# Full-row second matmul for the neighbourhood scores, and modulation sums on the vector engine

## The chip, the cores and the metric

The kernel runs on one core of a Trainium2 chip. The metric is device time in microseconds (us) of one execution, median of several runs. The core's engines work side by side, each through a queue of its own in order: PE (TensorE, matmuls; "PEld" is its weight load), DVE (VectorE), ACT (ScalarE), POOL (GpSimd) and SP (which here only issues transfers). They wait for each other by semaphores.

## The reference

One layer of a diffusion backbone over 512 latent tokens and 256 context tokens of 1024 channels. Cut to what the change touches:

```python
sh1, sc1, g1, sh2, sc2, g2 = adaln(c, w_mod, b_mod)      # split of silu(c) @ w_mod + b_mod, w_mod 1024 x 6144
hx = modulate(rmsnorm(x, norm_attn_g), sh1, sc1)         # the first 2048 columns: shift and scale
...
# neighbourhood attention, 8 heads of 64: window of 8 x 16 tokens with a learned bias, and all context keys
s = einsum('bqhd,bjkhd->bhqjk', qr, kr) * scale + bias   # masked outside the window
s_ctx = einsum('bqhd,bchd->bhqc', qr, k_ctx) * scale
p = softmax(concatenate([s, s_ctx]))
...
x = x + g1 * mixed                                       # columns past 2048: g1, sh2, sc2, g2
hx2 = modulate(rmsnorm(x, norm_ffn_g), sh2, sc2)
x = x + g2 * hierarchical_moe(hx2, ...)
```

## The kernel before

The program runs in stages: norms and projections of the tokens (to about 113 us), neighbourhood attention in four pairs of heads (p = 0 to 3, to about 268 us), latent attention, output projection with router, then 16 experts whose weights stream in, and the last norm. Up to the experts a scheduler sets the order of the instructions on each engine from the order of the code and its own estimates; the experts' order is written by hand.

**Neighbourhood scores.** A pair has 2 heads (u) and 4 blocks of 128 queries (i), 32 blocks in all. Matmuls in full precision are made of high and low parts: `qh` holds the high part of a head's queries twice (rows 0 to 63 and 64 to 127), `kk` the keys' high part (rows 0 to 63) and low part (rows 64 to 127). So the first matmul of `na_scores` (L599) gives high x high + high x low over 128 rows, and the second (L600) adds low queries x high keys over 64 rows, `ql[0:64]` and `kk[0:64]`. A block's 512 columns come in one to three pieces. DVE then adds the mask (L605) and takes the row maximum (L469), ACT takes the exponent (L612), PE transposes the weights (L621), DVE or ACT copies them (L81, L83). Scores have two banks in turn. Between these steps PE works off the projections of the next pair (`pull`: L56 to L58, three matmuls for each product), in pair 3 the latent heads' values.

**Modulation sums.** `mod_rest(n)` runs after every second block, 16 times: it loads two tiles `raw` of `w_mod_b` (128x1024 each, a ring of three buffers that the weights `w_qk`, `w_ukv` and `w_uq` share, all issued on SP) and lets PE add the product of 128 rows of silu(c) (`sstat`, 32 columns of which one counts) with 4 x 512 columns to a bank, in four groups of 32 columns of the array (L520). After 8 calls a row of 2048 columns is complete; DVE adds the bias (L524), SP stores it to `mod_d`. The latent attention's stage reads the gate g1 from there first.

Of the kernel before, what the change touches and what calls it, by code (L numbers as in the profile page):

```python
# [13 lines left out]
OP = mybir.AluOpType  # L14
# [16 lines left out]
# columns of the constant pack  # L31
# [6 lines left out]
def hybrid_kernel(tc, nc, x_k, x_q, ctx, cvec, w_mod_a, w_mod_b, b_mod_c, b_mod_r, g_ffn_row,  # L38
# [25 lines left out]
    # low parts that wait for their turn on the vector engine  # L64
# [22 lines left out]
    def rstd_steps(out, ss, n, n_cols, wk, first=None):  # L87
        """1 / sqrt(ss / n + eps): the root of the scalar engine, and one Newton step on its inverse.
        Of a sum in two parts the first one comes earlier."""
# [25 lines left out]
    # ------------------------------------------------------------ constants and small parameters  # L115
# [31 lines left out]
    # ------------------------------------------------------------ pools of the first phases  # L147
# [4 lines left out]
    # the tokens come in the places of the attentions' results  # L152
# [12 lines left out]
    # the root's table, ahead of its use  # L165
# [35 lines left out]
    def bank(*nums):  # L201
        """A bank of the sums' memory, of those named in turn."""
        n = taken[nums] = taken.get(nums, -1) + 1
        return psA.tile([P, 512], F32, name="ps", tag=f"b{nums[n % len(nums)]}", bufs=1)
# [8 lines left out]
    # ------------------------------------------------------------ modulated norm of the tokens, channel-major  # L213
# [24 lines left out]
    def mod_sums(q):  # L238
        """Shift and scale of two channel tiles, for latent and context tokens."""
# [14 lines left out]
    def mod_first(c):  # L254
        """The same of one of the first two channel tiles."""
# [90 lines left out]
    # ------------------------------------------------------------ latents of keys and values, of queries  # L346
# [30 lines left out]
    # what leaves for the memory lies apart from what follows  # L377
# [49 lines left out]
    # ------------------------------------------------------------ ring of the experts' weights  # L427
# [17 lines left out]
    def load_experts(n, behind=None):  # L445
        """Starts the loads of the next n chunks of experts' weights, in the order of their use."""
        for i in range(len(loads), min(len(loads) + n, len(order))):
# [6 lines left out]
            # few in flight, so that the small transfers between them don't queue for long  # L454
# [7 lines left out]
    # ------------------------------------------------------------ neighbourhood attention  # L462
# [3 lines left out]
    def row_max(s):  # L466
        """A block's row maximum, negated."""
        nm = cst.tile([P, 1], F32, name="nm", tag="nm", bufs=8)
        ve.tensor_reduce(out=nm, in_=s, axis=AX.X, op=OP.max, negate=True)  # L469
        return nm  # L470

    def softmax_block(s, pr, ssum):
        """exp of a block of scores less their row maximum, and the row sums."""
        ac.activation(pr, s, AF.Exp, bias=row_max(s), accum_out=ssum)

    def normalise_steps(ssum, wk, hi, lo):
        """Divides a pair of heads' sums by their rows' sums, which are turned into rows on the way."""
# [21 lines left out]
    # the sums of the experts' rows, by tokens  # L499
# [4 lines left out]
    # the other modulations, as rows  # L504
    mod_d = tc.dram_tile([2, 4, 512], F32, name="mod_d")
    modf = mod_d.rearrange("r a b -> r (a b)")
    mod_ps = []

    def mod_rest(n):
        r, k = divmod(n, KT)  # L510
        if k == 0:
            br = nw.tile([P, 512], F32, name="br", tag="br", bufs=1)
# [3 lines left out]
            mod_ps[:] = bank(7), br, rows  # L516
        ps, br, rows = mod_ps
        ws = [load(w_mod_b[r, k, :, q * 1024:(q + 1) * 1024]) for q in range(2)]
        for g in range(4):
            pe.matmul(ps[g * 32:(g + 1) * 32, :], sstat[:, k, :],  # L520
                      ws[g // 2][:, g % 2 * 512:g % 2 * 512 + 512], start=(k == 0), stop=(k == KT - 1),
                      tile_position=(0, g * 32))
        if k == KT - 1:
            ve.tensor_tensor(br, br, ps, op=OP.add)  # L524
            sy.dma_start(mod_d[r], rows)

    na_heads, na_w, na_ps = {}, {}, {}

    def na_open(p):
        heads = na_heads[p] = []  # L530
        for u in range(2):
            qh = nw.tile([P, T], F32R, name="qh", tag="qh", bufs=4)
            ql = nw.tile([P, T], F32R, name="ql", tag="ql", bufs=4)
# [9 lines left out]
    def na_bias(p, u):  # L543
        """The bias of a head, with the window's mask."""
# [4 lines left out]
    def na_weights(p, j, i):  # L549
        """The high part (i = 0) and the low one (1) of the weights of queries (j = 0) or keys (1)."""  # L550
# [8 lines left out]
    def na_project(p, j):  # L559
        """Queries (j = 0), latent keys (1) or context's keys (2) of a pair of heads. Yields between the steps."""  # L560
# [9 lines left out]
    def na_part(p, j, u, i):  # L570
        """Their high part (i = 0) and low one (1), of a head."""
# [16 lines left out]
    def na_scores(p, u, i):  # L588
# [9 lines left out]
        for o, n, c in pieces:  # L598
            pe.matmul(s[:, o:o + n], qh[:, qs], kk[:, c:c + n], start=True, stop=False)  # L599
            pe.matmul(s[:, o:o + n], ql[0:64, qs], kk[0:64, c:c + n], start=False, stop=True)  # L600
# [13 lines left out]
    def na_turn(p, u, i):  # L614
        """A block's weights by keys."""
# [32 lines left out]
    # ------------------------------------------------------------ latent attention  # L648
# [9 lines left out]
    def mla_values(t):  # L658
        """Values of the latent heads, and the queries' weights and latents in two parts. Yields between the steps."""
# [29 lines left out]
    for j in range(3):  # L689
        for n, _ in enumerate(na_project(0, j)):  # L690
# [4 lines left out]
            if n == 4 and j == 1:  # L695
                na_weights(1, 0, 0)
                na_weights(1, 0, 1)
                # the table of exp, ahead of its use
# [102 lines left out]
    def halves(n):  # L801
        """Two banks for sums of 1024 columns, by halves."""
# [11 lines left out]
    def k_rope(b):  # L814
        """The part of the keys that the heads share."""
        split_later(khs[b][64:96, :], kls[b][64:96, :], krt[64:96, :])

    def queries(a, ts=range(4)):
        """Queries of four heads."""
# [18 lines left out]
    def k_prep(p, hf):  # L838
        """Keys of a pair of heads, of the latent tokens (hf = 0) or the context's (1)."""
# [1058 lines left out]
```

## Time and profile before

| | |
|---|---|
| median of 3 runs | 760.02 us (759.91 to 760.87) |
| span of the profiled execution | 759.4 us |
| PE busy | 721.5 us (95%) |
| DVE busy | 546.4 us (72%) |
| ACT busy | 446.0 us (59%) |
| POOL busy | 77.8 us (10%) |

The span runs from the first to the last instruction of one profiled execution; the median of the runs without a profile is 0.6 us above it. Busy shares are over the whole span; they differ by stage, which the rows further down show. A record's length holds an engine's latency too, so instructions of one engine that follow each other closely overlap in the rows: what an instruction costs is the distance from its start to the next one's start. Rows of windows give the engines in the order PE, PEld, DVE, ACT, POOL.

### The profile page before, as it was taken

How to read it: one execution, taken by the hardware profiler on the slowest of the kernel's cores; microseconds unless marked ns; L12 is line 12 of the kernel's file. 1: busy time of each engine (PE TensorE's matmuls, PEld its weight loads, DVE VectorE, ACT ScalarE, POOL GpSimd, SP SyncE). 2: the span in 40 equal slices, each digit the busy share in tenths (PEclk: the TensorE clock that was granted, in tenths of full speed). 3: DMA queues.
4: the chain of work that ended last, by engine and by line, in shares of the span. 5: the costliest groups of instructions: out<-in, count | busy, mean ns of one | idle time of the engine just before them, and what ended most of it. 6: DMA issues, size and time to landing. Idle time of an engine off the chain costs nothing. (4 is left out here: it accounts for less than half of the span.)

```text
span 759.4 us, 10561 instructions
## 1 busy us (share of the span) xinstructions
PE 721.5 (95%) x3982; PEld 527.0 (69%) x3983; DVE 546.4 (72%) x744; ACT 446.0 (59%) x697; POOL 77.8 (10%) x46
## 2 busy tenths in 40 slices
PE   4999999999999999999999929999999999999995
PEld 4679987666665588776666826777777777777773
DVE  5572465646565589474564758999999999999996
ACT  6452364444434466464583428777777777777773
POOL 1000000000000000000000001033222322221220
PEclk9999999999999999999999958999999999999998
DMA  8931237544446662031139968999999999999872
GB/s 324 406 99 49 83 131 244 187 146 146 140 140 220 182 227 85 28 112 42 43 144 345 339 231 309 351 377 371 356 361 367 368 354 359 364 355 384 309 131 110
DMA packets 39621, 176.94 MB, mean 233 GB/s; under 512 B 5288, under 2 KB 6768, under 8 KB 27280
## 3 DMA queue, kind: packets, MB, share of 16 engines
q1 hardware_dynamic: 35168, 164.24, 58.6%
q0 software_dynamic: 4112, 11.92, 7.4%
q8 instruction: 32, 0.52, 0.3%
q14 instruction: 21, 0.17, 0.1%
q10 hardware_dynamic: 288, 0.08, 0.0%
HBM read 163.00 MB, written 15.32 MB: 235 GB/s over the span
## 5 line engine op out<-in xcount | busy, mean ns | idle before, releaser
L1356 DVE TENSOR_TENSOR el<-ew,eh 128x2048 fp32r<-128x2048 f32 (+1 forms) x106 | 220.5, 2087 | 20.7 <-ACT eh L1353 13.4
L1353 ACT CAST eh<-ew 128x1024 fp32r<-128x1024 f32 x190 | 189.7, 1048 | 43.2 <-PE s L58 28.6
L56 PE MATMUL s<-eh,xh 128*96 128x512 f32 x260 | 104.4, 401 | 0.9 <-ACT xh L61 0.9
L58 PE MATMUL s<-eh,xl 128*96 128x512 f32 x260 | 102.8, 396 | 0.0
L57 PE MATMUL s<-el,xh 128*96 128x512 f32 x260 | 102.4, 394 | 0.0
L1567 POOL DMA_INDIRECT ya_d<-yo,idx x14 | 45.5, 3253 | 140.4 <-DVE yo L1571 140.4
L58 PEld LDWEIGHTS s<-eh,xl 128*96 128x96 f32 x260 | 42.2, 162 | 19.1 <-DVE xl L62 0.6
L56 PEld LDWEIGHTS s<-eh,xh 128*96 128x96 f32 x260 | 42.2, 162 | 17.9 <-ACT xh L61 1.2
L57 PEld LDWEIGHTS s<-el,xh 128*96 128x96 f32 x260 | 42.3, 163 | 17.3 <-DVE el L1356 0.2
L56 PE MATMUL y<-eh,ghh 128*96 128x512 f32 x120 | 48.2, 401 | 0.0
L58 PE MATMUL y<-eh,ghl 128*96 128x512 f32 x120 | 47.3, 394 | 0.0
L57 PE MATMUL y<-el,ghh 128*96 128x512 f32 x120 | 47.2, 393 | 0.0
L56 PE MATMUL ps<-wh,hh 128*128 128x512 f32 (+2 forms) x128 | 43.8, 345 | 0.4 <-ACT hh L274 0.3
L469 DVE TENSOR_REDUCE nm<-s 128x1 f32<-128x768 f32 x32 | 30.5, 954 | 19.0 <-PE s L58 18.7
L58 PE MATMUL ps<-wh,hl 128*128 128x512 f32 (+2 forms) x128 | 43.5, 345 | 0.3 <-DVE hl L276 0.3
L57 PE MATMUL ps<-wl,hh 128*128 128x512 f32 (+2 forms) x128 | 43.3, 341 | 0.0
L1284 POOL MEMSET xg<- 128x1024 f32 x2 | 1.8, 950 | 388.0 <-DMA g<-mod_d 388.0
L605 DVE TENSOR_TENSOR ps<-ps,bb 128x256 f32<-128x256 f32 x32 | 13.8, 432 | 35.1 <-PE ps L600 35.0
L56 PE MATMUL ps<-hh,wh 128*128 128x512 f32 (+1 forms) x96 | 38.7, 403 | 0.0
L1242 POOL DMA_INDIRECT xg<-hx_d,idx x16 | 23.6, 1475 | 118.9 <-DVE va L1165 50.5
L933 ACT ACTIVATE pr<-s,nm 128x768 f32<-128x768 f32 x32 | 29.0, 908 | 9.6 <-DVE nm L469 9.3
L58 PE MATMUL ps<-hh,wl 128*128 128x512 f32 (+1 forms) x96 | 34.5, 359 | 0.0
(357 smaller groups left out, 1501.4 us busy)
## 6 DMA issues: line engine op xcount, KB each, us to landing
ew<-w_gate SPq DMA_DIRECT2D x32, 1024.0 KB, 9.3
ew<-w_up SPq DMA_DIRECT2D x32, 1024.0 KB, 9.2
ew<-w_down SPq DMA_DIRECT2D x32, 1024.0 KB, 9.3
raw<-w_mod_b SPq DMA_DIRECT2D x32, 512.0 KB, 3.8
wm<-w_mod_a SPq DMA_DIRECT2D x16, 512.0 KB, 9.2
raw<-w_qk SPq DMA_DIRECT2D x8, 512.0 KB
ya_d<-zero SPq DMA_DIRECT2D x10, 256.0 KB, 7.5
raw<-w_v SPq DMA_DIRECT2D x4, 512.0 KB
```

The source lines that it names most:

```text
L56: pe.matmul(ps, lh, rh, start=start, stop=False)
L57: pe.matmul(ps, lh, rl, start=False, stop=False)
L58: pe.matmul(ps, ll, rh, start=False, stop=stop)
L469: ve.tensor_reduce(out=nm, in_=s, axis=AX.X, op=OP.max, negate=True)
L605: ve.tensor_tensor(s[:, 0:256], s[:, 0:256], bb[:, 1 if i == 3 else 0, :], op=OP.add)
L933: ac.activation(pr, s, AF.Exp, bias=nm, accum_out=mla_ssum[h // 2][:, t, h % 2:h % 2 + 1])
L1242: ins = gp.indirect_dma_start(out=xg[e % NX][slice(0, CAP), :], out_offset=None, in_=hx_d, in_offset=bass.IndirectOffsetOnAxis(ap=idx[slic ...
L1284: gp.memset(x_, 0.0)
L1353: ac.copy(wh[:, cs], r[:, cs])
L1356: ve.tensor_tensor(wl[:, cs], r[:, cs], f(wh[:, cs]), op=OP.subtract)
L1567: gp.indirect_dma_start(out=ya_d, out_offset=bass.IndirectOffsetOnAxis(ap=idx[rows, 1, e:e + 1], axis=0), in_=yo[rows, :], in_offset=None, ...
```

## The change

Two edits. First, the low parts of the queries get four buffers of their own, `qls`, whose rows 64 to 127 POOL sets to zero once, and the second matmul of the scores runs over all 128 rows of `ql` and `kk` (L617 in the new numbering; the zeros cancel the keys' low part). Second, the columns of `w_mod` past 2048 are laid out in eight groups of 512. For each group DVE multiplies the 8 row tiles with their value of silu(c) by row and adds them up in `macc` (L529, L531), two half groups to the 16 calls; then four small matmuls with a matrix of ones (L535) sum over the rows, DVE adds the bias (L537) and SP stores 512 columns. `br` is 128 columns wide in place of 512, and `mod_d` is written eight times in place of two. The comments of the file went, too.

```diff
-    mod_d = tc.dram_tile([2, 4, 512], F32, name="mod_d")
-    modf = mod_d.rearrange("r a b -> r (a b)")
+    mod_d = tc.dram_tile([8, 4, P], F32, name="mod_d")
+    modf = mod_d.rearrange("(h r) a b -> h (r a b)", h=2)
     mod_ps = []
+    macc = nw.tile([P, 512], F32, name="macc")
+    ones = nw.tile([P, 32], F32, name="ones")
+    ve.memset(ones, 1.0)
 
     def mod_rest(n):
-        r, k = divmod(n, KT)
-        if k == 0:
-            br = nw.tile([P, 512], F32, name="br", tag="br", bufs=1)
+        r, h = divmod(n, 2)
+        if h == 0:
+            br = nw.tile([P, P], F32, name="br", tag="br", bufs=1)
             ve.memset(br, 0.0)
             rows = br.rearrange("(a b) n -> a b n", b=32)[:, 0, :]
             sy.dma_start(rows, b_mod_r[r])
-            mod_ps[:] = bank(7), br, rows
-        ps, br, rows = mod_ps
-        ws = [load(w_mod_b[r, k, :, q * 1024:(q + 1) * 1024]) for q in range(2)]
-        for g in range(4):
-            pe.matmul(ps[g * 32:(g + 1) * 32, :], sstat[:, k, :],
-                      ws[g // 2][:, g % 2 * 512:g % 2 * 512 + 512], start=(k == 0), stop=(k == KT - 1),
-                      tile_position=(0, g * 32))
-        if k == KT - 1:
-            ve.tensor_tensor(br, br, ps, op=OP.add)
+            mod_ps[:] = br, rows
+        br, rows = mod_ps
+        for k2 in (2 * h, 2 * h + 1):
+            w = load(w_mod_b[r, k2])
+            for i in range(2):
+                k = 2 * k2 + i
+                wk = w[:, i * 512:i * 512 + 512]
+                if k == 0:
+                    ve.tensor_scalar(macc, wk, sstat[:, k, 0:1], None, op0=OP.mult)
+                else:
+                    ve.scalar_tensor_tensor(macc, wk, sstat[:, k, 0:1], macc, op0=OP.mult, op1=OP.add)
+        if h:
+            ps = bank(7)
+            for g in range(4):
+                pe.matmul(ps[g * 32:(g + 1) * 32, 0:P], ones, macc[:, g * P:(g + 1) * P], start=True, stop=True,
+                          tile_position=(0, g * 32))
+            ve.tensor_tensor(br, br, ps[:, 0:P], op=OP.add)
             sy.dma_start(mod_d[r], rows)
...
+    qls = [nw.tile([P, T], F32R, name=f"ql{n}") for n in range(4)]
+    for ql in qls:
+        gp.memset(f(ql[64:128, :]), 0.0)
...
-            ql = nw.tile([P, T], F32R, name="ql", tag="ql", bufs=4)
+            ql = qls[(2 * p + u) % 4]
...
-            pe.matmul(s[:, o:o + n], ql[0:64, qs], kk[0:64, c:c + n], start=False, stop=True)
+            pe.matmul(s[:, o:o + n], ql[:, qs], kk[:, c:c + n], start=False, stop=True)
...
-    a["w_mod_b"] = c(wm[:, 2048:].reshape(KT, P, 2, 2048).transpose(2, 0, 1, 3))
+    a["w_mod_b"] = c(wm[:, 2048:].reshape(4, 2, P, 8, 512).transpose(3, 0, 2, 1, 4).reshape(8, 4, P, 1024))
...
-    a["b_mod_r"] = c(bm[2048:].reshape(2, 4, 512))
+    a["b_mod_r"] = c(bm[2048:].reshape(8, 4, P))
```

How this stands in the queues is seen at two places in pair 2. On PE before, at the end of the pair, a call's four matmuls of 512 columns follow the transposes of a block, ahead of the first scores of pair 3 (`c_58` is the unit matrix, `pr` the weights of a block):

```order
L600 MATMUL ps<-kk,ql 128x256
L621 MATMUL ps<-c_58,pr 128x128 x4
L520 MATMUL ps<-raw,sstat 32x512 x4
L599 MATMUL ps<-kk,qh 128x256
```

Now, at the same pair's second head, four matmuls of 128 columns follow the transposes, once for 8 row tiles, and wait for DVE's `macc`:

```order
L617 MATMUL ps<-kk,ql_1129 128x256
L56 MATMUL ps<-hh,wh 128x256
L57 MATMUL ps<-hl,wh 128x256
L58 MATMUL ps<-hh,wl 128x256
L638 MATMUL ps<-c_58,pr 128x128 x4
L535 MATMUL ps<-macc,ones 32x128 x4
```

The reading of `raw` has left PE's queue, and a short matmul on a sum from DVE has come into it. On DVE before, a stretch of the second head of pair 2 (mask add, maximum, low part of the next pair's keys `kk`):

```order
L81 COPY pt<-ps 128x512 [waits PE_49]
L546 TENSOR_TENSOR bb<-rb,cka 128x256 [waits DMAHW7_49]
L605 TENSOR_TENSOR ps<-ps,bb 128x256 [waits PE_49]
L469 TENSOR_REDUCE nm<-ps 128x1 [waits DVE_49]
L605 TENSOR_TENSOR ps<-ps,bb 128x256 [waits PE_49,Activation_49]
L584 TENSOR_TENSOR kk<-ps,kk 64x512 [waits Activation_49]
```

The same stretch now:

```order
L81 COPY pt<-ps 128x512 [waits PE_49]
L531 SCALAR_TENSOR_TENSOR macc<-raw,sstat,macc 128x512 [waits DMAHW3_49]
L622 TENSOR_TENSOR ps<-ps,bb 128x256 [waits PE_49,Activation_49]
L531 SCALAR_TENSOR_TENSOR macc<-raw,sstat,macc 128x512 [waits DVE_49]
L469 TENSOR_REDUCE nm<-ps 128x1 [waits DVE_49]
L531 SCALAR_TENSOR_TENSOR macc<-raw,sstat,macc 128x512 [waits DMAHW5_49,DVE_49]
L564 TENSOR_TENSOR bb<-rb,cka 128x256
L531 SCALAR_TENSOR_TENSOR macc<-raw,sstat,macc 128x512 [waits DVE_49]
L622 TENSOR_TENSOR ps<-ps,bb 128x256 [waits PE_49,Activation_49]
L601 TENSOR_TENSOR kk<-ps,kk 64x512 [waits Activation_49]
L537 TENSOR_TENSOR br<-br,ps 128x128 [waits DMAHW4_49,PE_49]
```

Four passes over `macc` stand between the steps of the scores, one between a mask add and its maximum, and the bias add behind them waits for PE.

## Rows read from the trace of the kernel before

**Rows 1.** Windows: us; busy us and instructions of each engine; granted clock; DMA; GB/s.
```profile
113.00:123.00 10.00, 10.00 (x57) 8.61 (x55) 7.18 (x13) 5.59 (x10) 0.00 (x0) 1.00 0.86 302
123.00:154.08 31.08, 31.08 (x162) 20.21 (x161) 18.60 (x35) 13.40 (x30) 0.00 (x0) 1.00 0.55 174
154.08:190.60 36.52, 36.52 (x214) 24.00 (x212) 19.81 (x34) 15.86 (x33) 0.00 (x0) 1.00 0.45 152
190.60:227.00 36.40, 36.40 (x212) 23.69 (x210) 19.90 (x37) 15.65 (x33) 0.00 (x0) 1.00 0.43 139
227.00:257.00 30.00, 30.00 (x157) 16.51 (x157) 18.05 (x31) 15.35 (x33) 0.00 (x0) 1.00 0.59 200
257.00:268.00 11.00, 11.00 (x79) 7.81 (x78) 4.50 (x8) 4.47 (x9) 0.00 (x0) 1.00 0.77 250
268.00:396.00 128.00, 124.83 (x724) 95.76 (x723) 87.64 (x140) 77.25 (x151) 1.84 (x2) 1.00 0.24 86
460.00:755.00 295.00, 291.07 (x1368) 206.13 (x1366) 276.09 (x205) 219.72 (x254) 69.74 (x31) 1.00 0.94 332
```

**Rows 2.** Waits of PE, then DVE, 115 to 290 us: total us, times, longest.
```profile
PE s L56 <- DVE q L835: 0.9, 1, 0.9
...
DVE ps L605 <- PE ps L600: 35.0, 24, 3.4
DVE wl L557 <- ACT wh L554: 8.0, 3, 3.8
...
DVE rsb L488 <- ACT rsb L487: 5.9, 2, 3.4
```

**Rows 3.** Timeline of PE from 122.77 us: start us, us, instruction.
```profile
122.77 0.40 PE L58 MATMUL ps<-hh,wl 128*128 128x512 f32 x1
123.00 0.28 PE L599 MATMUL ps<-kk,qh 128*128 128x256 f32 x1
123.21 0.38 PE L600 MATMUL ps<-kk,ql 64*128 64x256 f32 x1
123.52 0.50 PE L56 MATMUL ps<-hh,wh 128*128 128x512 f32 x1
123.85 0.39 PE L57 MATMUL ps<-hl,wh 128*128 128x512 f32 x1
```

**Rows 4.** Timeline of PE from 144.52 us.
```profile
144.52 1.06 PE L520 MATMUL ps<-raw,sstat 128*32 128x512 f32 x8
145.52 0.38 PE L56 MATMUL ps<-hh,wh 128*128 128x256 f32 x1
145.74 0.28 PE L57 MATMUL ps<-hl,wh 128*128 128x256 f32 x1
145.86 0.28 PE L58 MATMUL ps<-hh,wl 128*128 128x256 f32 x1
```

**Rows 5.** Timeline of PE from 149.42 us, a block of three pieces.
```profile
149.42 0.22 PE L599 MATMUL ps<-kk,qh 128*128 128x128 f32 x1
...
151.30 0.40 PE L57 MATMUL ps<-hl,wh 128*128 128x512 f32 x1
```

**Rows 6.** Instructions by tile (ql, sstat): ns min/median/max, first and last start, forms.
```profile
L600 PE MATMUL ps<-kk,ql x64: 322/380/502, 123.2 to 254.0; 64*128 64x256 f32 x40, 64*128 64x128 f32 x16, 64*128 64x512 f32 x8
L520 PE MATMUL ps<-raw,sstat x128: 592/605/617, 127.0 to 259.2; 128*32 128x512 f32 x128
```

**Rows 7.** DVE groups by shape (busy us, mean ns, idle before); two passes on the timeline.
```profile
L275 DVE SCALAR_TENSOR_TENSOR xnt<-xnt,ab,hh 128x576 f32<-128x576 f32 x8 | 6.4, 814 | 1.9 <-ACT hh L274 1.9
L276 DVE TENSOR_SCALAR hl<-xnt,ab 128x576 fp32r<-128x576 f32 x8 | 4.0, 515 | 0.1
L275 DVE SCALAR_TENSOR_TENSOR xnt<-xnt,ab,hh 128x256 f32<-128x256 f32 x8 | 3.8, 479 | 0.7 <-ACT hh L274 0.7
...
31.17 1.54 DVE L275 SCALAR_TENSOR_TENSOR xnt<-xnt,ab,hh 128x576 f32<-128x576 f32 x2
```

**Rows 8.** Timeline of PE, the first modulation sums.
```profile
42.39 0.42 PE L245 MATMUL ps<-wm,sstat 128*32 128x128 f32 x6
```

## Prediction

> **What bounds the kernel now.** I read the busy shares by stage first, since the change lies in one stage only. [rows 1] cuts the span at the places where the neighbourhood heads' work begins and ends: 113 us (last projections before the first scores), 123.00, 154.08, 190.60 and 227 (first scores of the four pairs of heads), 257 and 268 us (end of the neighbourhood heads). In each of these six windows PE (TensorE) is busy the whole time, at a granted clock of 1.00, while DVE (VectorE) is busy 7.18, 18.60, 19.81, 19.90, 18.05 and 4.50 us, together 88.0 us of 155. Then I read who waits for whom [rows 2]: PE waits 0.9 us for anybody between 115 and 290 us; DVE waits 35.0 us for the second scores' matmul alone. So PE sets the pace of this stage, and DVE has 67 us to spare. The two later windows of [rows 1] are as full on PE (124.83 of 128 us and 291.07 of 295 us), and their instructions keep their order: what the stage gains or loses reaches the end nearly whole.
>
> **PE, the second scores' matmul.** L600 multiplies 64 rows, its neighbours 128. In [rows 3] full matmuls follow each other every 0.23 us (512 columns, 122.77 to 123.00). L599 starts at 123.00 with 256 columns, L600 only 0.21 us later, the next full one 0.31 us after that, and the one behind it 0.33 us later, since its weights, too, were not loaded ahead. From 123.00 to 123.85 is 0.85 us. Three matmuls of 256, 256 and 512 columns, all full, would take 0.12 + 0.12 + 0.23 = 0.47 us (0.12 from 145.74 to 145.86 in [rows 4]). So a pair loses 0.38 us at the change to 64 rows and back. [rows 5] has two pairs of 128 columns, one of 256 and one full 512: 1.88 us against 6 x 0.12 + 0.23 = 0.95, a loss of 0.93, of which 0.38 is the 256 pair's, so 0.28 for each 128 pair. The counts are in [rows 6]: 40 pairs of 256, 16 of 128, 8 of 512, which I price like 256: 48 x 0.38 + 16 x 0.28 = 22.7 us of PE time that filling the rows would free. The zeros cost one POOL memset of 64x512 for each of four buffers. POOL has nothing else to do in this stage [rows 1] and can clear them as soon as their memory is free, ahead of the first scores: nothing. (If that memory came free late, the first scores of pair 0 would wait, once.)
>
> The Trainium skill weighs against this edit: TensorEngine Tiling (Array Packing), Performance Considerations, counts a contraction of 64 rows as a case for row tiling, two tiles at a time and up to twice as fast, which filling up to 128 rows gives away. By that rule the 64 pieces would each stream at most their 0.12 us longer and nothing would come back. The trace doesn't show such a pairing: each L600 in [rows 3, 5] stands alone between 128-row matmuls. By the rows it is 22.7 us less for PE, by the rule up to 8 us more.
>
> **PE, the modulation sums.** A call of the old code is four matmuls of 32x512 (eight records); in [rows 4] from 144.52 to 145.74, less the 0.12 us of the matmul behind it, 1.10 us. There are 16 calls ([rows 6]: 128 records): 17.6 us. In their place come eight groups of four matmuls with 128 columns. [rows 8] has six records of that shape in 0.42 us; eight of them and the change of shape I take as 0.55 us: 4.4 us. PE's sum: 155 - 22.7 - 17.6 + 4.4 = 119 us.
>
> **DVE, what it takes over.** 64 new passes over 128x512: 8 products (tensor_scalar) and 56 product-and-adds (scalar_tensor_tensor, two tensors and a scalar by row). The nearest rows are L275, the same kind with scalars by row, all in SBUF: 479 ns at 256 columns, 814 at 576 [rows 7], so 1.05 ns a column and 0.75 us at 512. Two of them take 1.54 us together, the second adding 0.73, 0.08 less than its record: 0.66 us each where they run back to back. The products are nearest to L276, 515 ns at 576 columns: 0.40 us. 56 x 0.66 + 8 x 0.40 = 40.2 us; the smaller bias sums (8 of 128 columns for 2 of 512) and their memsets add under 1. With whole records it is 56 x 0.75 + 8 x 0.52 = 46 us. I take 41, since most have another instruction between them. DVE then needs 129 us where PE needs 119: **DVE becomes the bound of the stage**, and the gain is not PE's 36 us.
>
> By window, with 10 us of new work for each pair of heads (two sums, 14 adds and 2 products), of which the order puts six passes (3.7 us) ahead of the first scores:
> - to the first scores: 7.2 + 3.7 = 10.9, so 11 us (10 before)
> - pair 0: 18.6 + 6.3 = 24.9 (31.1 before)
> - pair 1: 29.8 (36.5); pair 2: 29.9 (36.4); pair 3 up to 257 us: 28.1 (30.0)
> - the end, bound by PE's chain of values, transposes and normalising: 11 less half a call, 10.5
>
> Together 134.2 us: the floor, with DVE never waiting. Two things come on top. A pass that needs the sum just made waits for its end, 0.1 us more; about half do: 3 us. And waits that no new pass can stand in for: 35.0 of DVE's 67 idle us are for scores that PE will now have ready, but the waits for the high part of the next weights (8.0 us, the longest 3.8) and for the sums turned into rows (5.9 us) [rows 2] sit behind a load into the ring of three buffers, a cast and PE's transposes. I keep half of 13.9 us: 7. The stage: 134.2 + 3 + 7 = 144 us, 11 less than before. The profiled span 759.4 becomes 748.5; the median of the runs is 0.6 above it: **749 us**.
>
> What else moves: the ring's buffers are now given back by DVE in place of PE, on SP's queue. Each load of w_mod_b waits for two passes of the tile three loads earlier, and eight small stores of the finished rows and eight small loads of the bias stand between, where two of each stood. Behind such a store SP holds the next weights' load. In the order, some ten DVE instructions (5 to 7 us) lie between the pass that frees a buffer and the one that reads what is loaded there, about what a load and a cast need; this is why I keep half of those waits and don't strike them. Each sum's four matmuls wait for DVE, and DVE's bias add waits for them, with one or two instructions between: hidden while PE is the faster one.
>
> **Rivals.**
> 1. *DVE packs almost without waits.* For it: over half of its idle time is the scores' wait, and PE gets 36 us of slack to run ahead. Then the stage takes the floor of 134 to 138 us: 739 to 743 us. Chance 0.13.
> 2. *Slower: the new passes delay the scores' own chain.* Mask add and row maximum share DVE's queue with the passes, in order, up to four passes between one mask add and the next; exp, transposes and copies hang on the maximum, and PE stands in its queue at the transposes. If none of the 32 us of waits that are not for scores goes away, the stage takes 88 + 41 + 32 = 161 us: 766 us; with whole records 771. It decides once DVE's waits in the stage pass 155 - 129 = 26 us, the point of no gain. Against it: scores of the next block stand ahead of the transposes in PE's queue, so a late maximum doesn't starve DVE of its next input. Chance 0.20.
> 3. *The rows aren't filled to any use:* 128-row matmuls with zeros as slow as the 64-row ones. PE keeps 155 - 13.2 = 142 us, DVE's 129 fit in below it with fewer waits filled, the stage takes some 148 us: 752 us. Against it: the full matmuls' own spacing in [rows 3, 4]. Chance 0.07. If the Trainium skill's rule on row tiling above held in full, it would be up to 8 us more, 760 us.
> 4. *No change:* DVE's waits come out near the 26 us of rival 2, the two edits cancel: 758.5 to 761.5 us. Chance 0.08.
>
> The clock is no rival with a chance of its own: PE would be busy some 80% of the stage, and no window of [rows 1] shows less than 1.00.
>
> **How the numbers follow.** The forecast (743 to 757 us, that is 10 to 24 us of waits on DVE in the stage) gets the remaining 0.52. The range of 8 in 10 leaves out the lowest part of rival 1 (under 742) and the upper part of rival 2 (over 763): 742 to 763 us. Faster by more than 0.2%, about what a measurement of this kernel can tell: 0.52 + 0.13 + 0.07 = 0.72; within 0.2%: 0.08; slower: 0.20. The forecast's own range is 743 to 757.
>
> **What would show it.** Right: between the first scores and the end of the neighbourhood heads DVE's busy share goes from 57% to about 90%, PE's falls to about 80%, PE now waits for DVE (at the four sum matmuls and, by way of exp, at the transposes); the gap before the second scores' matmul goes, and two matmuls of 256 columns start 0.12 us apart; a pass of 128x512 has a record near 0.75 us; the later stages keep their length. Wrong: L617 still starts 0.2 us behind L616 (rival 3); a pass of more than 0.85 us; DVE idle for more than 26 us in the stage, behind loads of the ring, weights' casts or PE's transposes (rival 2); or a later stage that takes the gain back, above all the first latent heads, which need the gate row that the sums write.

## The result, and the profile after

| | before | after |
|---|---|---|
| median of the runs compared | 759.96 us (759.78 to 760.87, 4 runs) | 750.6 us (748.81 to 751.77, 3 runs) |
| span of the profiled execution | 759.4 us | 750.0 us |
| stage of the neighbourhood heads, 113 us to the first `s<-uq` matmul behind it | 153.7 us (to 266.71) | 143.8 us (to 256.82) |

The ratio is 0.9877, with a 95% interval from 0.9853 to 0.9901: faster, by 9.3 us. A fourth run of the changed kernel, 1151 us at a mean clock of 0.56, is left out here; with it the median is 751.2 us, the figure on record for the prediction.

The first view is the changed kernel by windows, with the columns of [rows 1]: the two halves of the stage (cut at the first mask addition of head pair 2), the whole stage, and all that comes behind it. After that come the four places where the granted clock fell, each with the stretch ahead of it.

```profile
113.00:179.63 66.63, 64.62 (x409) 52.05 (x408) 61.53 (x115) 34.55 (x71) 0.00 (x0) 1.00 0.61 207
179.63:256.82 77.19, 62.18 (x392) 43.67 (x391) 62.69 (x117) 34.73 (x71) 0.00 (x0) 0.91 0.55 174
...
113.00:256.82 143.82, 126.80 (x798) 95.72 (x797) 124.22 (x230) 69.28 (x142) 0.00 (x0) 0.95 0.58 189
256.82:750.00 493.18, 466.62 (x2365) 340.51 (x2363) 401.43 (x454) 323.15 (x452) 74.33 (x36) 0.97 0.74 262
...
188.00:191.90 3.90, 1.53 (x9) 0.89 (x7) 3.90 (x7) 3.87 (x7) 0.00 (x0) 0.97 0.46 149
191.90:195.30 3.40, 3.10 (x8) 2.43 (x9) 3.06 (x6) 1.93 (x5) 0.00 (x0) 0.53 0.85 273
...
208.00:212.40 4.40, 2.06 (x16) 1.45 (x15) 4.28 (x10) 1.48 (x4) 0.00 (x0) 0.97 0.70 239
212.40:215.80 3.40, 3.40 (x15) 1.92 (x17) 3.40 (x6) 0.92 (x2) 0.00 (x0) 0.54 0.56 149
225.00:236.30 11.30, 5.46 (x36) 3.92 (x34) 10.54 (x17) 5.56 (x11) 0.00 (x0) 0.99 0.67 210
236.30:239.70 3.40, 3.40 (x12) 1.66 (x8) 3.33 (x8) 1.20 (x4) 0.00 (x0) 0.54 0.64 208
244.00:249.90 5.90, 2.13 (x20) 1.23 (x20) 5.60 (x11) 3.19 (x8) 0.00 (x0) 0.98 0.52 166
249.90:253.40 3.50, 3.50 (x28) 2.69 (x28) 0.75 (x2) 0.62 (x1) 0.00 (x0) 0.54 0.87 259
```

Where [rows 1] had PE busy in every microsecond, PE now idles 17.0 us of the stage (143.82 less 126.80) and DVE 19.6 us. What lies behind the stage takes 493.18 us against 492.7 before: the gain is the stage's. And the stage has two halves. Up to 179.63 us PE is busy 97% of the time at full clock. In pairs 2 and 3 it idles 15 of 77.19 us, and the clock is not 1.00: four times it falls from 2.4 to 1.2 GHz (granted clock 0.5) for 3.4 us, each time behind a stretch in which, as it is cut here, PE was busy for 1.53 of 3.90 us, 2.06 of 4.40, 5.46 of 11.30 and 2.13 of 5.90, while DVE was busy nearly throughout.

Next the waits of the same stretch, 113 to 256.82 us, as in [rows 2]: PE, then DVE, then ACT.

```profile
PE ps L535 <- DVE macc L531: 5.3, 2, 3.2
PE ps L638 <- ACT pr L629: 4.5, 7, 1.6
PE ps L616 <- ACT pr L629: 2.6, 2, 2.3
PE ps L58 <- DVE wl L574: 1.4, 1, 1.4
PE ps L56 <- ACT wh L571: 1.2, 1, 1.2
...
DVE rsb L488 <- ACT rsb L487: 5.6, 1, 5.6
DVE br L537 <- PE ps L535: 4.3, 3, 3.0
DVE ps L622 <- PE ps L617: 2.4, 5, 1.0
...
ACT pr L629 <- DVE nm L469: 31.8, 24, 2.9
```

DVE's wait for the second scores' matmul, 35.0 us in [rows 2], is down to 2.4. In its place PE waits for DVE: at once, at the sums' matmuls (5.3 us), and by way of ACT, whose exponential `pr` waits 31.8 us for DVE's row maxima `nm` (18.9 us before) and lets PE's transposes (L638) and scores (L616) wait 7.1 us in turn.

The third view is PE's timeline at the first scores, which answers to [rows 3].

```profile
120.15 0.28 PE L616 MATMUL ps<-kk,qh 128*128 128x256 f32 x1
120.27 0.28 PE L617 MATMUL ps<-kk,ql 128*128 128x256 f32 x1
120.39 0.27 PE L616 MATMUL ps<-kk,qh 128*128 128x256 f32 x1
120.50 0.28 PE L617 MATMUL ps<-kk,ql 128*128 128x256 f32 x1
```

The new passes by line: ns least/median/most, first and last start, forms.

```profile
L531 DVE SCALAR_TENSOR_TENSOR macc<-raw,sstat,macc x56: 626/743/752, 116.9 to 248.3; 128x512 f32<-128x512 f32 x56
L529 DVE TENSOR_SCALAR macc<-raw,sstat x8: 356/477/484, 115.7 to 237.0; 128x512 f32<-128x512 f32 x8
```

The full-row matmuls follow each other every 0.12 us, where [rows 3] had 0.21 and 0.31. A pass takes 743 ns.

What a fall of the clock does, and what comes ahead of one, shows on PE's timeline and DVE's at the first of them (in brackets: the idle time before, and whom it waited for).

```profile
190.02 0.50 PE L56 MATMUL ps<-hh,wh 128*128 128x512 f32 x1 [1.23 <-ACT wh L571]
190.36 0.40 PE L57 MATMUL ps<-hl,wh 128*128 128x512 f32 x1
192.20 0.79 PE L58 MATMUL ps<-hh,wl 128*128 128x512 f32 x1 [1.45 <-DVE wl L574]
192.79 0.63 PE L56 MATMUL ps<-hh,wh 128*128 128x512 f32 x1
193.22 0.63 PE L57 MATMUL ps<-hl,wh 128*128 128x512 f32 x1
...
188.69 0.73 DVE L531 SCALAR_TENSOR_TENSOR macc<-raw,sstat,macc 128x512 f32<-128x512 f32 x1
189.33 0.68 DVE L490 TENSOR_TENSOR onl<-rsb,onh 128x512 fp32r<-128x512 f32 x1
189.93 0.74 DVE L531 SCALAR_TENSOR_TENSOR macc<-raw,sstat,macc 128x512 f32<-128x512 f32 x1
190.60 0.42 DVE L622 TENSOR_TENSOR ps<-ps,bb 128x256 f32<-128x256 f32 x1
190.93 1.21 DVE L574 TENSOR_TENSOR wl<-raw,wh 128x1024 fp32r<-128x1024 f32 x1
```

PE first waits 1.23 us for ACT's cast `wh` of the next weights and then 1.45 us for their low part `wl`, which DVE makes from `wh`. PE's first matmul with `wh` starts at 190.02 us; DVE begins `wl` at 190.93, behind one more pass and a mask addition. Once PE runs again, matmuls of 512 columns stand 0.43 us apart (192.79 to 193.22) instead of the 0.23 us of [rows 3].

### The profile page after: what moved, and what is told of

The parts are those of the page before. It is cut to its first block, busy times and chain, and to the rows that moved or that the text cites. A ratio compares the mean times of both kernels' runs of the same rounds, so it can differ in the third digit from the quotient of the medians.

```text
span 750.0 us, 10572 instructions
## 1 busy us (share of the span) xinstructions
PE 694.7 (93%) x3918; PEld 522.8 (70%) x3919; DVE 584.0 (78%) x821; ACT 446.6 (60%) x697; POOL 79.5 (11%) x50
## 4 chain that ended last, share of the span: by engine, by line
PE 81%; DVE 8%; ACT 4%; DMA 4%; issue 2%; SPq 0%; DVEq 0%; ACTq 0%
PE s L56 11%; PE s L58 11%; PE s L57 11%; PE ps L58 5%; PE ps L56 4%; PE ps L57 4%; PE y L58 4%; PE y L56 4%; PE y L57 4%; PE o L972 3%; PE ps L647 3%; PE tr L963 3%; DVE macc L531 2%; PE t L1515 1%; DMA xb<-x_k 1%
## 5 line engine op out<-in xcount | busy, mean ns | idle before, releaser
L56 PE MATMUL s<-eh,xh 128*96 128x512 f32 x260 | 104.6, 402 | 0.9 <-ACT xh L61 0.9
L57 PEld LDWEIGHTS s<-el,xh 128*96 128x96 f32 x260 | 42.5, 163 | 17.4 <-DVE el L1373 0.2
L531 DVE SCALAR_TENSOR_TENSOR macc<-raw,sstat,macc 128x512 f32<-128x512 f32 x56 | 41.2, 736 | 0.6 <-DMA raw<-w_mod_b 0.5
L629 ACT ACTIVATE pr<-ps,nm 128x512 f32<-128x512 f32 x32 | 22.0, 689 | 32.7 <-DVE nm L469 31.8
L56 PE MATMUL ps<-hh,wh 128*128 128x512 f32 (+1 forms) x96 | 35.8, 373 | 1.7 <-ACT wh L571 1.2
```

The source lines that it names most:

```text
L56: pe.matmul(ps, lh, rh, start=start, stop=False)
L57: pe.matmul(ps, lh, rl, start=False, stop=False)
L531: ve.scalar_tensor_tensor(macc, wk, sstat[:, k, 0:1], macc, op0=OP.mult, op1=OP.add)
```

## The experiments

Twelve kernels, each compared with the kernel before on the same chip (the median is of 4 runs, of 10 for e2, e5 and e10, of 3 for the changed kernel). "Stage" is from 113 us to the first `s<-uq` matmul in the profiled execution, with PE and DVE busy and the mean granted clock in it.

| kernel | median us | ratio to before (95%) | stage us | PE | DVE | clock |
|---|---|---|---|---|---|---|
| before | 759.96 | | 153.7 | 153.7 | 87.4 | 1.00 |
| after | 750.6 | 0.9877 (0.9853 to 0.9901) | 143.8 | 126.8 | 124.2 | 0.95 |
| e1 full rows alone | 740.7 | 0.9739 (0.9702 to 0.9776) | 134.2 | 131.2 | 85.7 | 1.00 |
| e2 sums on DVE alone | 764.3 | 1.0052 (1.0032 to 1.0071) | 157.8 | 148.0 | 124.3 | 0.94 |
| e3 every second row of sums on PE | 738.4 | 0.9702 (0.9666 to 0.9739) | 131.9 | 124.3 | 104.6 | 0.99 |
| e4 sums on POOL | 810.0 | 1.0653 (1.0616 to 1.0689) | 204.1 | 138.8 | 96.6 | 0.83 |
| e5 after, 16 more passes on DVE | 757.6 | 0.9974 (0.9952 to 0.9996) | 152.5 | 129.8 | 134.6 | 0.91 |
| e6 after, 15.6 us more on PE | 745.4 | 0.9806 (0.9775 to 0.9838) | 139.0 | 133.5 | 124.0 | 0.99 |
| e7 last four rows of sums on PE | **734.9** | 0.9688 (0.9646 to 0.9729) | 128.5 | 125.1 | 105.3 | 1.00 |
| e8 after, sums' matmuls a block later in the code | 751.2 | 0.9878 (0.9843 to 0.9913) | 145.5 | 130.0 | 123.8 | 0.92 |
| e9 after, more on PE in the last 8 calls | 747.8 | 0.9834 (0.9810 to 0.9859) | 141.2 | 129.0 | 123.5 | 0.98 |
| e10 e2 with the same | 761.2 | 1.0018 (1.0000 to 1.0036) | 152.5 | 147.3 | 124.5 | 1.00 |
| e11 last three rows of sums on PE | 741.3 | 0.9740 (0.9704 to 0.9777) | 131.5 | 124.9 | 109.7 | 0.99 |
| e12 after, half a call behind every block | 746.9 | 0.9837 (0.9811 to 0.9862) | 138.8 | 123.3 | 122.6 | 0.96 |

Two things limit what a single pair of these can show. A scheduler orders the stage from the code and its own estimates, so most edits also move other instructions. And a stage is that of one execution: e3's profiled one took 743.4 us where its median is 738.4; the time behind the stage lies between 490.9 us (e12) and 496.7 us (e3); and the cut at 113 us falls at slightly different places in the work (the first cast of pair 0's weights starts between 97.8 and 99.1 us). Differences between stages of less than about 2 us are not to be read.

### Each edit alone, a mix, and a third engine

e1 is the kernel before with the change's `qls` and the full rows:

```diff
-                pe.matmul(s[:, o:o + n], ql[0:64, qs], kk[0:64, c:c + n], start=False, stop=True)
+                pe.matmul(s[:, o:o + n], ql[:, qs], kk[:, c:c + n], start=False, stop=True)
```

> The kernel before with the full rows of the neighbourhood scores' second matmul alone; the modulation sums stay on TensorE. Theory (the recorded sum): the 64-row form cost 48x0.38 + 16x0.28 = 22.7 us of TensorE in the stage, TensorE goes from 155 to about 132 us and stays the bound there, VectorE stays at about 88 us of work, no stretch of the stage shows a clock under 1.00: 736 to 741 us. Rival (the rows that are filled with zeros buy nothing): 758 to 762. Rival (VectorE's waits grow instead): 745 to 752.

e2 is the changed kernel with this line as it was. 

> The changed kernel with the second matmul back on 64 rows: the modulation sums on VectorE alone. Theory: TensorE loses 17.6 us and gets 4.4 us back, 155 to about 142 us; VectorE has about 125 us; the passes lie partly in the 35 us in which VectorE waited for the second matmul: 747 to 754 us, TensorE's clock 1.00 in nearly all of the stage. Rival (the passes are the whole loss, VectorE late with everything behind them): 758 to 775.

e3 is the changed kernel with the odd rows of sums in matmuls of 32x128 that add up in a bank, as the kernel before does it:

```diff
+                if r % 2:
+                    for g in range(4):
+                        pe.matmul(ps[g * 32:(g + 1) * 32, 0:P], sstat[:, k, :], wk[:, g * P:(g + 1) * P],
+                                  start=(k == 0), stop=(k == KT - 1), tile_position=(0, g * 32))
-                if k == 0:
+                elif k == 0:
```

> The changed kernel, with every second row of modulation sums (4 of 8) back on TensorE: full rows, and half of the VectorE passes. Theory (VectorE is the bound of the changed kernel's stage and TensorE's clock dips because it waits): TensorE about 119 + 6.6 = 126 us, VectorE 125 - 18 = 107 us, no stretch under clock 1.00: 731 to 738 us, faster than either edit alone. Rival (what the changed kernel lost is in the chain of waits and not in VectorE's sum): 745 to 751. Rival (rows alone stay best): slower than e1_rows_only by over 1 us.

e4 gives the passes to POOL:

```diff
-                    ve.scalar_tensor_tensor(macc, wk, sstat[:, k, 0:1], macc, op0=OP.mult, op1=OP.add)
+                    gp.tensor_scalar(wk, wk, sstat[:, k, 0:1], None, op0=OP.mult)
+                    gp.tensor_tensor(macc, macc, wk, op=OP.add)
```

> The changed kernel with the modulation sums on GpSimd instead of VectorE, each of the 64 passes as a product in place and an addition. Theory (VectorE's passes are the bound): VectorE falls from 125 to about 85 us in the stage and TensorE bounds it at about 119 to 125 us, 724 to 733 us, if one pass pair on GpSimd stays under 2.0 us (64 x 2.0 = 128 us of a 145 us stage) and does not slow VectorE. Rival (GpSimd is slower than that, and its sums come late): the stage follows GpSimd, 64 x 3 us = 192 us, 780 us or more. Rival (the two engines hold each other up): VectorE's operations in the stage are longer by over 10% in the mean, 740 to 770 us.

**Measured.** The full rows alone take 740.7 us, as the theory had it: 10 us better than the change as a whole. Its stage in the windows:

```profile
113.00:247.22 134.22, 131.15 (x861) 93.72 (x859) 85.71 (x153) 68.01 (x141) 0.00 (x0) 1.00 0.63 202
```

In e1 PE has 22.6 us less to do (153.71 less 131.15) and is still the bound, with 3.1 us idle: the theory's figure, and the rival that zeros buy nothing has fallen. The sums alone were a miss. They cost 4 us where a gain of 6 to 13 was expected, which is the range of the rival that has the passes as the whole loss; the clock is 0.94 in the mean, which is some 19 us at half of it (0.06 x 157.8, twice). So the change is one edit that gains 19.5 us of stage and one that gives 9.6 back on top of it. Moving only half of the sums (e3) gives 738.4, a little above its theory's 731 to 738, with one fall of the clock left. Its four runs (736.2 to 743.4) overlap e1's (739.2 to 741.8), so that it beats the rows alone is not shown.

In e4 POOL is the bound, as its groups by shape show (busy us, mean ns, idle time before); below them two of DVE's groups in e4, and then the first of these two in the changed kernel, where its line is L563:

```profile
L531 POOL TENSOR_SCALAR raw<-raw,sstat 128x512 f32<-128x512 f32 x55 | 88.6, 1624 | 22.6 <-DMA raw<-w_mod_b 20.4 <-DMA rb<-rel 2.2
L532 POOL TENSOR_TENSOR macc<-macc,raw 128x512 f32<-128x512 f32 x56 | 74.8, 1336 | 2.9
...
L564 DVE TENSOR_TENSOR bb<-rb,cka 128x256 f32<-128x256 f32 x8 | 7.3, 915 | 0.0
L623 DVE TENSOR_TENSOR ps<-ps,bb 128x256 f32<-128x256 f32 x32 | 13.6, 425 | 21.6 <-PE ps L618 21.5
...
L563 DVE TENSOR_TENSOR bb<-rb,cka 128x256 f32<-128x256 f32 x8 | 3.3, 415 | 0.0
```

A product and an addition take 2.96 us there against 0.74 on DVE. Of the stage's 204.1 us POOL is busy for 173.4 and waits another 20.4 for its loads. That is the first rival's case, 810.0 us where it said 780 or more: the slower engine sets the stage. The sign of the other rival is there too: DVE without the passes is busy 96.6 us, against 85.7 in e1.

### What bounds the changed kernel: more work for one engine at a time

e5 adds a pass that multiplies by zero at the end of each of the 16 calls, e6 four matmuls of 32x384 whose sums nothing uses:

```diff
+        ve.scalar_tensor_tensor(macc, wk, zero[:, 0:1], macc, op0=OP.mult, op1=OP.add)
```

```diff
+        for g in range(4):
+            pe.matmul(ps[g * 32:(g + 1) * 32, P:512], sstat[:, k, :], wk[:, P:512], start=True, stop=True,
+                      tile_position=(0, g * 32))
```

> The changed kernel with one more pass of VectorE in each of the 16 calls, which multiplies by zero and adds nothing (128x512, about 0.75 us, 12 us in all). Theory (VectorE, with the waits that it sets, bounds the changed kernel's stage): 757 to 764 us, the stage 7 to 12 us longer. Rival (TensorE or the chain between the engines bounds it, VectorE has 19 us of idle time that takes the passes): 750 to 753 us.

> The changed kernel with four more matmuls of 32x384 in each of the 16 calls (about 0.9 us a call, 14 us in all; their sums are used by nothing). Theory (TensorE has about 17 us of idle time in the stage, and its clock dips to half because it idles): most of the work is hidden, fewer dips: 748 to 756 us. Rival (TensorE bounds the stage after all): 763 to 767 us. Rival (the dips alone cost what was lost): under 747 us.

**Measured.** 10.4 us more of DVE work make the stage 8.7 us longer. 15.6 us more of PE work make it 4.9 us *shorter*, 139.0 us, and the median falls to 745.4: DVE is what the stage follows, and an idle PE costs something. Neither is the added work alone: e5's mean clock of 0.91 is some 27 us at half clock where the changed kernel has 14, and e6 has another order of instructions. The two halves of e6:

```profile
113.00:180.85 67.85, 67.24 (x457) 50.78 (x455) 61.63 (x115) 35.17 (x71) 0.00 (x0) 1.00 0.60 202
180.85:251.95 71.10, 66.30 (x471) 43.83 (x470) 62.39 (x116) 35.08 (x73) 0.00 (x0) 0.98 0.56 184
```

DVE has the same work as in the changed kernel, 124.0 us. The first half, which had no fall of the clock to lose, is 1.2 us longer than the changed kernel's; the second, where one fall is left of four, is 6.1 us shorter. The run came out below the theory's 748 to 756, on the side of the rival that sees the whole loss in the clock; but 139.0 us is not yet e1's 134.2.

e9 and e10 put the extra matmuls only into the last eight calls (`for g in range(4 if r > 3 else 0)`), e9 on the changed kernel, e10 on e2.

> The changed kernel with the four extra matmuls of 32x384 (used by nothing) in the last 8 calls alone, where its clock dipped: 7.8 us of TensorE's time more (the 16 calls cost 15.6 us in the run before). Theory (the dips come from TensorE waiting, and cost about 5 us): the first half as in the changed kernel (pairs 0 and 1 in 58 us), the second half without dips or with one, 743 to 747 us. Rival (it was the different order of the bank for the sums, or chance, that made the run with 16 calls shorter): 749 to 753 us with the dips, or 757 and more with TensorE's extra work on top.

> The kernel with the sums on VectorE and the 64-row matmuls, with the same four extra matmuls (used by nothing) in its last 8 calls. Theory (what made that kernel slower than before, against the sum that said 750, was the half clock of its second half): the clock of the stage goes from 0.94 to 0.98 or more and the time to 754 to 760 us although TensorE has 7.8 us more to do. Rival (its loss is VectorE's passes on the path; the clock only follows): 763 to 768 us. Rival (TensorE bounds it at full clock too): 768 to 773.

**Measured.** The matmuls cost PE 6.8 us here. e9: two falls of the clock are left, and the stage is 2.7 us shorter in spite of them: 1.7 in the second half and 1.0 in the first, where the order of instructions is still the changed kernel's, so that this 1.0 is scatter and the place of the cut (the same work lies 0.7 us earlier in e9). At 747.8 us it missed the theory's upper end by 0.8. e10: no fall at all, where e2 spent about 20 us at half clock; the stage is 5.3 us shorter. The median falls by 3.1 us, less than expected (761.2, against 754 to 760): the half clock was part of e2's miss, not all of it. The stages of the changed kernel, e9 and e6 stand in the order of their falls, four, two and one: 143.8, 141.2, 139.0 us; these are three executions with three orders of instructions, not a measurement of the clock alone.

### Where the passes and the sums stand

e8 puts the sums' four matmuls and DVE's addition behind the next block's mask addition in the code, instead of directly behind the last pass (a function `mod_finish()`, called behind `na_max`). e12 runs half a call behind every block instead of a whole one behind every second:

```diff
-        if i % 2:
-            mod_rest(p * 4 + u * 2 + i // 2)
+        mod_rest(b)                     # one load, two passes; k2 = b % 4, the sum at k2 == 3
```

> The changed kernel with the four matmuls over macc and VectorE's addition behind them issued one block later, after the next block's scores and mask; the passes stay. Theory (VectorE's own work bounds the stage, the 5.3 us wait of TensorE for macc and the 4.3 us wait of VectorE for its sums are added on top): 742 to 748 us, both waits gone. Rival (the waits only move to the next thing that VectorE is late with): 749 to 752.

> The changed kernel with the passes spread evenly: two behind every block of scores in place of four behind every second one, the same 64 passes and eight sums. Theory (it is not VectorE's sum of work, 124 us in a stage of 144, but four passes at a stretch ahead of what TensorE and ScalarE wait for, and the dips that follow): the stage 134 to 140 us, 740 to 747 us, ScalarE's wait for the row maxima under 12 us in place of 17.4 in the second half. Rival (the sum of VectorE's work with its fixed waits sets the stage): 749 to 753 us. Rival (the later sums, or two loads at other times, cost more): over 754.

**Measured.** e8 takes 751.2 us, and it is no test of its theory, because the scheduler undid the edit. Only the first of the eight sums moved behind the next block's scores; the other seven stand in PE's and DVE's queues where the changed kernel has them. The last sum in the changed kernel, then in e8, and after that e8's waits at the sums and its stage:

```profile
249.06 0.43 PE L535 MATMUL ps<-macc,ones 128*32 128x128 f32 x8 [2.05 <-DVE macc L531]
249.66 5.35 PE L647 MATMUL ps<-pt,nav 128*64 128x512 f32 x38 [0.17 <-DVE pt L81]
...
250.73 0.43 PE L542 MATMUL ps<-macc,ones 128*32 128x128 f32 x8 [1.97 <-DVE macc L531]
251.33 5.35 PE L654 MATMUL ps<-pt,nav 128*64 128x512 f32 x38 [0.17 <-DVE pt L81]
...
PE ps L542 <- DVE macc L531: 4.0, 2, 2.1
...
DVE br L544 <- PE ps L542: 4.9, 3, 3.6
...
113.00:258.49 145.49, 129.96 (x796) 99.23 (x794) 123.75 (x228) 68.71 (x140) 0.00 (x0) 0.92 0.57 187
```

What the waits at the sums cost stays untested. e8 serves as a second execution of nearly the same order instead: it spent some 23 us at half clock where the changed kernel spent 14, and its stage is 1.7 us longer.

e12 hit: 746.9 us, the stage 5.0 us shorter with the same 64 passes and two falls of the clock, one of them 6.8 us long. ACT's wait for the row maxima is 24.2 us in place of 31.8, and 9.6 in place of 17.4 in the second half. On DVE of the changed kernel up to five passes stand between two mask additions, and in pair 3 three passes once, and four once, between a mask addition and its own maximum; in e12 it is at most three and at most one. So where the passes stand matters, and not only their sum.

### The split that the halves suggest

e7 leaves the first four rows of sums on DVE, where PE was 97% busy, and gives the last four back to PE, as in e3 with `r > 3`. e11 moves the border by one row, `r > 4`.

> The changed kernel with the last four of the eight rows of sums back on TensorE (the second half of the stage, where TensorE idled and its clock dipped), the first four on VectorE (where TensorE was 97% busy). Theory (the loss of the changed kernel lies in the second half, and its gain in the first): 113 to 182.7 us as in the changed kernel, the rest of the stage 60 to 64 us as with every second row on TensorE: 734 to 739 us, no stretch below clock 1.00. Rival (it is only the sum of VectorE's passes that counts): as with every second row, 737 to 740. Rival (the first half does not gain from it): 741 or more.

> Five rows of sums on VectorE and the last three on TensorE (four and four gave 734.9). Theory (the third of the four head pairs is bound by TensorE at 31.8 us there and VectorE has 22.2, so a row moved to VectorE takes 2.2 us off and gives 0.6 back): 733 to 735 us. Rival (VectorE's waits come back in that pair, the clock dips): 736 to 740.

**Measured.** e7 is the fastest of all, 734.9 us: 3.1% below the kernel before and 16 us below the change, as the theory had it. (The expectations' 182.7 us lies one block of scores behind the middle of the stage; the rows here are cut at the middle.) Its two halves, and then those of e1:

```profile
113.00:179.20 66.20, 64.42 (x408) 51.85 (x407) 61.29 (x115) 34.30 (x70) 0.00 (x0) 1.00 0.62 207
179.20:241.52 62.32, 60.68 (x616) 46.10 (x615) 43.96 (x85) 33.89 (x71) 0.00 (x0) 1.00 0.64 213
```

```profile
113.00:179.00 66.00, 66.00 (x433) 50.06 (x432) 44.54 (x81) 34.05 (x71) 0.00 (x0) 1.00 0.65 211
179.00:247.22 68.22, 65.15 (x431) 43.66 (x429) 41.17 (x73) 33.96 (x71) 0.00 (x0) 1.00 0.60 194
```

Up to the middle all three stand alike (changed kernel 66.63, e7 66.20, e1 66.00 us). The sums that PE need not make there don't shorten that half; PE uses part of the time to run ahead with the next pairs' projections. Its groups up to 180 us count 45 first matmuls of 512 columns in e7 and 41 in e1:

```profile
L56 PE MATMUL ps<-hh,wh 128*128 128x512 f32 x45 | 18.2, 404 | 0.5 <-DVE kk L604 0.5
```

```profile
L56 PE MATMUL ps<-hh,wh 128*128 128x512 f32 x41 | 17.3, 422 | 0.0
```

So the gain of e7 over e1 falls due in the second half, where PE has 60.7 us to do instead of 65.2, and DVE is free to keep up. In the changed kernel it is taken from PE there as well, but DVE, with 62.7 us of work, can't follow: 77.2 us. One more row on DVE (e11) loses 6 us, a little more than the rival's 736 to 740 us. In the profiled executions 2.9 us of that lie in the stage; the rest lies behind it (494.9 us, against 491.5 in e7), where nothing was changed. In the stage e11's windows have the same wait and the same fall as the changed kernel, at the same place:

```profile
188.00:191.20 3.20, 0.89 (x4) 0.30 (x2) 3.20 (x6) 3.17 (x6) 0.00 (x0) 1.00 0.56 170
191.20:194.60 3.40, 3.04 (x7) 2.37 (x8) 3.12 (x6) 1.99 (x5) 0.00 (x0) 0.51 0.83 280
```

It is there that the passes of row 4 stand ahead of the weights' low part.

## Why the prediction was right, and where it was not

The forecast was 749.0 us (742 to 763), the result is 751.2 (750.6 by the runs compared). Its steps:

| step of the prediction | forecast | measured |
|---|---|---|
| full rows free PE time | 22.7 us | 22.6 (e1) |
| sums leave PE, small ones come | 17.6 - 4.4 = 13.2 us | 13.2 (e10: 153.7 - 147.3 + 6.8) |
| PE's work after | 119 us | 126.8; an estimated 120 without the falls of the clock |
| a pass of 128x512 | 0.75 us by record | 0.743 us |
| DVE takes over | 41 us | 36.8 (124.2 - 87.4) |
| DVE idle in the stage | about 15 us | 19.6 |
| the stage is shorter by | 11 us | 9.9 |
| later stages | keep their length | 493.2 after 492.7 us |

**What held.** PE set the pace before, and the price of a 64-row matmul between 128-row ones, read from four starts on a timeline, was right to 0.2 us in 22.7. The rule in the Trainium skill, TensorEngine Tiling (Array Packing), Performance Considerations, which takes 64 rows for a case of 2x row tiling, is about two such tiles at a time; here, where each stands alone, e1 decides against leaving the rows empty. DVE became the bound, which e5 and e6 show from both sides: work for DVE lengthens the stage by 0.8 us for each microsecond (with more of it at half clock), work for PE doesn't. DVE's share of the stage is 86% (about 90% forecast) and PE's 88% (80% forecast).

**What failed** is the step "the clock is no rival with a chance of its own: PE would be busy some 80% of the stage". 80% as a mean says nothing of how the idle time lies: it lay in stretches like the four shown above, and behind these the clock went to 1.2 GHz. Of 13.7 us at half clock PE was busy 13.4; half of that, an estimated 6.7 us, is what PE's work grew by, the distance between 126.8 and 120. Most of it seems to have been hidden, since DVE was the bound: in e8, with nearly the same order, 10 us more at half clock went with 1.7 us more of stage. The Trainium skill, TensorE: Matmul & The Clock Gate, HAM oscillation, describes a kernel whose TensorE waits for its operands again and again and each time resumes at half clock; the trace agrees for these four stretches, behind which 512 columns take 0.43 us instead of 0.23 us. The prediction didn't weigh that page.

**What was mis-sized.** DVE's new work came out 4 us lower than the sum and its idle time almost 5 us higher; the two nearly cancel, so that the total is nearer than its parts is luck. Of the idle time, the 7 us kept for the next weights and the sums turned into rows were right: 0.8 and 5.6 us are left. What the sum lacks is mostly the bias addition's wait for the sums' matmuls, put at nothing ("hidden while PE is the faster one") and measured at 4.3 us, and DVE's shorter waits for scores and transposed weights (2.4 and 2.0 us). The ring of buffers cost DVE 0.5 us. The idle time is rival 2's mechanism in part: passes delay the row maxima (ACT waits 31.8 us for them, e1 15.6) and the weights' low part, and PE then stands still. It stayed under the 26 us from which that rival decides. e12 supports it: the same passes, spread out, give 5.0 us back, though with fewer falls of the clock and another order.

**What the prediction's own sums said and it didn't.** Full rows alone leave PE 155 - 22.7 = 132 us to do; with the sums moved the stage was forecast at 144. The second edit was a loss of 12 us by these numbers. Measured: 134.2 against 143.8, a loss of 9.6. The prediction added the edits up and never set one against the other.

**What stays open.** How the 9.6 us divide between the half clock and the delayed work. Filling PE brought 2.7 to 4.9 us back and spreading the passes 5.0, but each also changed the order and the number of falls. The one pair of nearly equal order, e8 and the changed kernel, puts the half clock's part at an estimated 2 to 3 us (1.7 us for 10 us, so 2.3 for 14; 3.2 if both stages are counted from the first cast of pair 0's weights); it is a single pair of executions. e2's loss isn't settled beyond the 5.3 us of stage that e10 took off.

## What to carry to other kernels

When a change has two edits, make the sum for each of them alone: an edit that takes work off the engine that is no longer the bound, and puts it on the one that is about to be, is a loss inside a gain. Give work to the second engine only in the stretches where the first is full (pairs 0 and 1 here), and spread it, so that what others wait for doesn't stand behind several passes. When the busiest engine stops being busy, look at where its idle time will lie: here TensorE's clock fell behind such stretches, and work that nobody needs (e6) made the kernel 5 us faster. And look in the queues whether an edit took effect: the scheduler undid e8's.

## What the runs showed of the hardware

- TensorE's clock fell to half after short stretches of partial idleness inside a stage that is 88% busy, and came back 3.4 us later in each of the four cases; e10, at 97% busy, had no fall, and e6, at 96%, had one. In e2 one stretch at half clock lasted 13.7 us.
- While POOL worked on the sums in e4, DVE's addition of two operands in SBUF (the bias of 128x256) took 915 ns in the mean (351 to 1515), against 415 ns in the changed kernel; the mask addition of the same size, with one operand in the matmuls' bank, stayed at 425 ns against 426. The Trainium skill, SBUF — State Buffer, SBUF: two separate sides, has the port pair that these two engines share, which an operation of DVE with two inputs in SBUF needs; these rows agree with it.
